# A two-layer hybrid encoder: down projection partly by seven block products, low weight products last in a block, wide weight tiles and one pool of general buffers

## The chip, the core and the metric

The kernel runs on one core of one Trainium2 chip, in one launch. The metric is device microseconds of one execution; the kernel before has a median of 1971.58 us over three runs (1971.37 to 1972.12). Engines are called TensorE (PE in the profile, its weight loads PEld), VectorE (DVE), ScalarE (ACT), GpSimd (POOL) and SyncE (SP).

## The reference

256 tokens of width 2048 go through two layers. Each layer normalises its rows, makes one input projection, runs windowed attention and a chunked spatial gate side by side, joins them by an output projection, and then runs a gated feed-forward part with a hidden width of 5632. All is float32. What the change concerns is the last line:

```python
def conv_gated_ffn(h, w_up, conv_w, conv_b, w_down):
    a = depthwise_conv_centred(h @ w_up, conv_w, conv_b)
    g, u = jnp.split(a, 2, axis=-1)
    return (jax.nn.silu(g) * u) @ w_down

x = x + conv_gated_ffn(rms_norm(x, norm2_g[l]), w_up[l], conv_w[l], conv_b[l], w_down[l])
```

## The kernel before

**Products in three parts.** TensorE multiplies in a rounded 32-bit format. To keep float32 accuracy, each operand is split into a rounded high part and the remainder, the low part, and a product is three matmuls into one PSUM sum: activation hi by weight hi, activation lo by weight hi, activation hi by weight lo. The activations (transposed, 128 x 128 for one of the two row halves m and one group of 128 channels k) are the operand that TensorE holds; 512 columns of weights stream past.

**A block.** The weights of every projection come as blocks of four k by 512 columns, 1 MB each. `split_weights` (L113) takes a raw tile from a pool of three, lets SyncE load it (L119), and has ScalarE copy it rounded into hi tiles (L127) and VectorE subtract these from raw into lo tiles (L111). Hi and lo tiles are 1024 wide, four of each; so each holds half a block, two blocks in all. `rows_by_cols` (L163) then issues 24 matmuls (L170): for each k four hi products (two row halves, activation hi and lo), then the two low products of the same k. In the very first blocks the raw tile is loaded in four pieces and split piece by piece.

**The feed-forward part.** `gate_and_up(j)` (L814) makes four k of the hidden activations: two sums of four blocks each, one for the gate and one for the up half. `leave` scales a finished sum, takes it apart into 16-bit halves, and SyncE transposes them by DMA (L809). Two `let_in` points later (there is one in each block, after its second k) the step after it runs: ScalarE puts the words together (L381, `together`), the convolution follows (L781 on ScalarE, L782 and L785 on VectorE), and for the up half the product with silu of the gate (L827) and the split of the hidden activations, `ys`, into hi (L242, ScalarE) and lo (L243, VectorE).

**The down projection.** The 44 k are handled in two parts, k 0 to 23 after six gate/up units, and k 24 to 43 after five more. In each part the four groups of 512 columns, c, come one after the other; each has a PSUM tile of two banks for the two row halves, goes through all blocks of the part, and is then added to the residual `xr` (`residual`, L560; in the last part of the last layer L872, from where it is written out). There are three such PSUM tiles (`mm`) and two of one bank (`tp`).

**What sets the order.** A scheduler places the instructions of each engine by priority and program order, and gives out pool buffers; splitting of weights is marked `urgent`, which lets it run as far ahead as buffers allow. On the chip each queue runs in its written order, and an instruction that reuses a buffer waits until the last reader of the old contents is done. General buffers: 58 slots `sl` of 512 words per partition, four `ev` and four `sc` of the same size.

## Time and profile before

| | before |
|---|---|
| median of three runs | 1971.58 us (1971.37 to 1972.12) |
| profiled execution | 1971.57 us, of which 1969.8 us are its span |
| granted TensorE clock | 1.000 |
| TensorE, busy | 1963.6 us |
| VectorE, busy | 1256.4 us |
| ScalarE, busy | 1316.6 us |
| bytes read | 378.43 MB |

The span reaches from the first to the last instruction of the profiled execution, and what lies around it is 1.8 us. Matmuls are pipelined: one takes 389 ns from its start to its end, while the next starts after less than 230, so busy time is the union and a rate is read from runs of matmuls. In a row of grouped instructions the two numbers behind the bar are busy time and the mean of one; "idle before" is what the engine stood still ahead of them.

### The profile page before, as it was taken

Reading aid. Unit: us, or ns where it says so; the run is one execution under the profiler, and the core shown is the slowest. Engines: PE = TensorE matmul, PEld = TensorE weight load, DVE = VectorE, ACT = ScalarE, POOL = GpSimd, SP = SyncE. Lnnn points to the kernel's source line nnn. Section 1 sums busy time; section 2 is a strip of 40 time slices with the busy share of each in tenths; the row PEclk is TensorE's granted clock in tenths of the full one; section 3 lists DMA queues with packets and bytes.
Section 4 is the critical chain, followed back from the end, with each engine's and each line's share of the span. In section 5 each row is a group of like instructions: output and inputs, shape, how many; then the busy total and the mean of one; then the engine's idle time right before and its main releaser. Section 6 shows DMA issues by size and latency. Waiting matters only on the chain.

```text
span 1969.8 us, 23916 instructions
## 1 busy us (share of the span) xinstructions
PE 1963.6 (100%) x8880; PEld 1630.6 (83%) x8880; DVE 1256.4 (64%) x1754; ACT 1316.6 (67%) x1685; POOL 22.6 (1%) x25
## 2 busy tenths in 40 slices
PE   9999999999999999999999999999999999999999
...
PEclk9999999999999999999999999999999999999999
...
GB/s 342 205 204 150 205 239 202 222 219 228 216 198 192 199 215 204 229 221 205 215 204 248 141 178 203 235 206 218 232 218 219 193 192 203 213 216 217 220 216 126
DMA packets 190741, 414.09 MB, mean 210 GB/s; under 512 B 139424, under 2 KB 140704, under 8 KB 145568
## 3 DMA queue, kind: packets, MB, share of 16 engines
...
q8 instruction: 69, 1.13, 0.2%
...
HBM read 378.43 MB, written 2.10 MB: 193 GB/s over the span
## 4 chain that ended last, share of the span: by engine, by line
PE 97%; DVE 2%; issue 0%; DMA 0%; SPq 0%; POOL 0%; ACT 0%; DVEq 0%
PE mm L170 91%; PE mm L211 2%; PE tp L170 1%; PE mm L216 1%; DVE lo L111 1%; PE tp L254 0%; PE tp L256 0%; PE tp L255 0%; PE tp L697 0%; PE tp L482 0%; DMA raw<-in_w_in 0%; DVE sl L235 0%; DVE xr L562 0%; SPq L87 0%; DVE sl L265 0%
## 5 line engine op out<-in xcount | busy, mean ns | idle before, releaser
L170 PE MATMUL mm<-hi,sl 128*128 128x512 f32 x5296 | 1418.4, 389 | 0.8 <-DVE sl L243 0.6
L111 DVE TENSOR_TENSOR lo<-raw,hi 128x1024 fp32r<-128x1024 f32 (+1 forms) x708 | 856.5, 1217 | 627.6 <-ACT hi L127 616.7
L170 PEld LDWEIGHTS mm<-hi,sl 128*128 128x128 f32 x5296 | 992.7, 188 | 208.2 <-DVE sl L243 1.5
L127 ACT ACTIVATE hi<-raw 128x1024 fp32r<-128x1024 f32 (+1 forms) x708 | 739.9, 1051 | 461.5 <-PE mm L170 426.0
L170 PE MATMUL mm<-lo,sl 128*128 128x512 f32 x2648 | 816.1, 389 | 0.0
L170 PEld LDWEIGHTS mm<-lo,sl 128*128 128x128 f32 x2648 | 496.9, 188 | 103.1
L381 ACT COPY sl<-sl 128x1024 uint16<-128x1024 uint16 x98 | 132.1, 1351 | 119.3 <-DMA sl<-sl 119.2
L781 ACT ACTIVATE sc<-sl,pc 128x256 f32<-128x256 f32 x176 | 97.0, 588 | 0.0
L801 ACT COPY sl<-ev 128x1024 uint16<-128x1024 uint16 x88 | 89.5, 1037 | 0.0
L782 DVE SCALAR_TENSOR_TENSOR sc<-sl,pc,sc 128x255 f32<-128x255 f32 x176 | 79.1, 479 | 2.6 <-ACT sc L781 2.6
L785 DVE SCALAR_TENSOR_TENSOR sc<-sl,pc,sc 128x255 f32<-128x255 f32 x176 | 79.1, 480 | 1.6
L211 PE MATMUL mm<-sl,hi 128*128 128x512 f32 x256 | 62.0, 391 | 0.0
L211 PEld LDWEIGHTS mm<-sl,hi 128*128 128x128 f32 x256 | 47.3, 188 | 9.3
L799 ACT ACTIVATE ev<-mm,yr 128x512 f32<-128x512 f32 x88 | 54.8, 672 | 0.0
L235 DVE SCALAR_TENSOR_TENSOR sl<-sl,pc 128x256 fp32r<-128x256 f32 x96 | 42.5, 479 | 16.9 <-ACT sl L234 16.9
L242 ACT ACTIVATE sl<-sl 128x256 fp32r<-128x256 f32 x88 | 32.1, 410 | 27.9 <-DVE sl L827 27.4
L234 ACT ACTIVATE sl<-sl,pc 128x256 fp32r<-128x256 f32 x96 | 43.0, 496 | 1.2 <-DMA pc<-in_pcol 0.6
L535 ACT COPY sl<-sl 128x1024 uint16<-128x1024 uint16 x24 | 32.4, 1349 | 6.8 <-DMA sl<-sl 6.8
L216 PE MATMUL mm<-sl,lo 128*128 128x256 f32 x256 | 34.2, 285 | 0.0
L243 DVE TENSOR_TENSOR sl<-sl 128x256 fp32r<-128x256 f32 x88 | 33.3, 419 | 0.0
L216 PEld LDWEIGHTS mm<-sl,lo 128*128 128x128 f32 x256 | 32.4, 191 | 0.6
L827 DVE TENSOR_TENSOR sl<-sl,sc 128x512 f32<-128x512 f32 x44 | 30.2, 686 | 0.2
...
## 6 DMA issues: line engine op xcount, KB each, us to landing
raw<-in_w_up SPq DMA_DIRECT2D x176, 1024.0 KB, 5.0
raw<-in_w_down SPq DMA_DIRECT2D x88, 1024.0 KB, 4.9
raw<-in_w_in SPq DMA_DIRECT2D x38, 1024.0 KB, 5.3
raw<-in_w_o SPq DMA_DIRECT2D x32, 1024.0 KB, 5.0
raw<-in_w_gu SPq DMA_DIRECT2D x16, 1024.0 KB, 5.1
sl<-sl SPq DMA_TRANSPOSE x244, 3.6
...
```

Source lines behind the costliest of these rows:

```text
L111: nc.vector.tensor_tensor(out=lo, in0=part, in1=hi.bitcast(F32), op=ALU.subtract)
L127: nc.scalar.activation(hi[:, cs], part, AF.Copy)
L170: nc.tensor.matmul(ps[m], acts[kk][:, part % 2, m * P : (m + 1) * P], w, start=first and kk == 0 and part == 0, stop=last and kk == KB - 1 ...
L211: nc.tensor.matmul(ps[:, i, :], tile_of(his, k, i), x1, start=k == 0, stop=False)
L216: nc.tensor.matmul(ps[:, i, :SEQ], tile_of(los, k, i), acts[k][:, 0, :], start=False, stop=k == NK - 1)
L234: nc.scalar.activation(t[:, 0, :], src, AF.Copy, scale=g)
L381: nc.scalar.copy(words, tall.rearrange("p (b a) n -> p b (a n)", b=2))
L781: nc.scalar.activation(t[:, i, :], s[:, i, :], AF.Identity, bias=col(3), scale=col(1))
L782: nc.vector.scalar_tensor_tensor(out=t[:, i, 1:], in0=s[:, i, : SEQ - 1], scalar=col(0), in1=t[:, i, 1:], op0=ALU.mult, op1=ALU.add)
L785: nc.vector.scalar_tensor_tensor(out=t[:, i, : SEQ - 1], in0=s[:, i, 1:], scalar=col(2), in1=t[:, i, : SEQ - 1], op0=ALU.mult, op1=ALU.add)
L799: nc.scalar.activation(rows, ps[:, m, :], AF.Copy, scale=r2[:, m : m + 1])
L801: nc.scalar.copy(h, rows.bitcast(U16).rearrange("p (j n b) -> p j b n", j=2, b=2))
```

## The change

**Seven products for eight.** Take two k (k0, k1), two column groups (c0, c1) and the two row halves: eight block products, 24 matmuls. In 20 places (ten per layer) of two k and two c each they are made by seven products of sums, 21 matmuls, in the scheme of Strassen and Winograd. `seven` loads the four 512-wide weight pieces as one raw tile; VectorE makes four sums of them in a second raw tile (three instructions); ScalarE makes hi parts of three pieces and of all sums, VectorE the low parts. `mixed` makes the four sums of activations on VectorE and splits them. Three of the seven products go into the PSUM sums of c0 and c1, and four kinds go into four extra sums `more` (one `mm` tile and both `tp` tiles), shared by all such blocks of a pair of c; `seven_out` adds these into `xr` at the end of the pair's last one.

**Where.** The parts are now k 0 to 19 (five gate/up units) and 20 to 43 (six). In the first part both pairs of c have such blocks at k 4, 8 and 14; in the second only the first pair has, at k 4, 8, 14 and 18 of the part. The two column groups of a pair now alternate block by block, and the seven-product block stands between them (the last one of the second part ahead of both).

**Elsewhere.** Hi and lo tiles are a whole block wide (2048), three hi and two lo; a block's 16 hi products come first and its eight low ones last; in the spatial gate's `unit` the low products go through k in the outer loop. `ev` and `sc` buffers come from the `sl` pool, which has 62. The weights of the down projection are laid out in the order of use.

The core of the diff:

```diff
+HALVES = ((0, 20), (20, NF))
+FAST = ((4, 8, 14), (4, 8, 14, 18))
...
-    slots = pool("slots", 58)
-    evp = pool("evp", 4)
+    slots = pool("slots", 62)
     rawp = pool("rawp", 3)
-    hip = pool("hip", 4)
-    lop = pool("lop", 4)
-    scr = pool("scr", 4)
+    hip = pool("hip", 3)
+    lop = pool("lop", 2)
...
+            hi, lo = hi_tile(), lo_tile()
+            for a in range(0, n, step):
+                cs = slice(a, min(a + step, n))
+                nc.scalar.activation(hi[:, cs], raw[:, cs], AF.Copy)
+                lo_part(lo[:, cs], raw[:, cs], hi[:, cs])
...
             for m in range(2):
                 product(m, kk, 0)
                 product(m, kk, 1)
-            for m in range(2):
-                product(m, kk, 2)
             if kk == 1:
                 let_in()
+        for kk in range(KB):
+            for m in range(2):
+                product(m, kk, 2)
...
+    def mixed(y):
+        t = y.rearrange("p a (m t) -> p (a m) t", t=P)
+        e = ev().rearrange("p a (m t) -> p (a m) t", t=P)
+        a21 = t[:, 1:2, :].to_broadcast([P, 2, P])
+        nc.vector.tensor_tensor(out=e[:, 0:2, :], in0=a21, in1=t[:, 0:4:3, :], op=ALU.subtract)
+        nc.vector.tensor_tensor(out=e[:, 2, :], in0=t[:, 0, :], in1=e[:, 1, :], op=ALU.subtract)
+        nc.vector.tensor_tensor(out=e[:, 3, :], in0=t[:, 2, :], in1=e[:, 2, :], op=ALU.subtract)
+        return parts(e.rearrange("p a t -> p (a t)"), [P, W])
+
+    def seven(left, right, more, acts, mix, src, used_left, used_right, first, last):
+        with urgent():
+            raw = raw_tile()
+            nc.sync.dma_start(raw, src)
+            sums = raw_tile()
+            hi, lo, his, los = hi_tile(), lo_tile(), hi_tile(), lo_tile()
+            nc.scalar.activation(hi[:, : 3 * W], raw[:, : 3 * W], AF.Copy)
...
+            nc.vector.tensor_tensor(out=s[:, 0:2, :], in0=b12, in1=b[:, 0:3:2, :], op=ALU.add)
+            nc.vector.tensor_tensor(out=s[:, 2, :], in0=s[:, 0, :], in1=b[:, 2, :], op=ALU.add)
+            nc.vector.tensor_tensor(out=s[:, 3, :], in0=s[:, 2, :], in1=b[:, 1, :], op=ALU.add)
+            nc.scalar.activation(his, sums, AF.Copy)
+            lo_part(lo[:, : 3 * W], raw[:, : 3 * W], hi[:, : 3 * W])
+            lo_part(los, sums, his)
...
+        product(left, used_left, 0, own(1, 0), (hi, lo), 1)
+        product(right, used_right, 0, mix_of(3), (hi, lo), 2)
+        product(more, used_more, 0, own(0, 0), (hi, lo), 0)
+        lows()
+        product(more, used_more, 1, mix_of(2), (his, los), 2)
+        product(more, used_more, 2, mix_of(1), (his, los), 0)
+        product(more, used_more, 3, mix_of(0), (his, los), 1)
+        product(left, used_left, 1, own(1, 1), (his, los), 3)
+        lows()
```

In the rows below, a name is a tile with its number, `out<-in`, and L is the line in the kernel that the rows are from: in the changed kernel L146 makes a low part, L253 to L255 the sums of weights, L238 to L240 those of activations, L367 the low part of these, L901 and L904 the convolution, L948 the product with the gate, L361 the low part of the hidden activations, L298 to L304 are `seven_out`, L678 is the residual, L213 a matmul of a plain block in the down projection, and L273, L274 and L279 are the hi and low matmuls of a seven-product block.

First, TensorE in layer 0 where the first part of the down projection has begun. Before, the first blocks of c0:

```order
L170 MATMUL mm_4683<-hi_4686,sl_3051 128x512 x4
L170 MATMUL mm_4683<-lo_4687,sl_3051 128x512 x2
L170 MATMUL mm_4683<-hi_4686,sl_3054 128x512 x4
L170 MATMUL mm_4683<-lo_4687,sl_3054 128x512 x2
L170 MATMUL mm_4683<-hi_4690,sl_3076 128x512 x4
L170 MATMUL mm_4683<-lo_4691,sl_3076 128x512 x2
L170 MATMUL mm_4683<-hi_4690,sl_3079 128x512 x4
L170 MATMUL mm_4683<-lo_4691,sl_3079 128x512 x2
```

Now, the first seven-product block, which follows the first plain block (lo_4051 is that plain block's low tile, hi_4089 and lo_4090 are the pieces, hi_4091 and lo_4092 the sums, sl_4027 and sl_4028 the mixed activations):

```order
L273 MATMUL mm_4047<-hi_4089,sl_3173 128x512
L274 MATMUL mm_4047<-hi_4089,sl_3173 128x512
L279 MATMUL mm_4047<-lo_4090,sl_3173 128x512
L273 MATMUL mm_4047<-hi_4091,sl_3173 128x512
L274 MATMUL mm_4047<-hi_4091,sl_3173 128x512
L279 MATMUL mm_4047<-lo_4092,sl_3173 128x512
L273 MATMUL mm_4082<-hi_4089,sl_4027 128x512
L273 MATMUL mm_4083<-hi_4089,sl_3170 128x512
L274 MATMUL mm_4083<-hi_4089,sl_3170 128x512
L279 MATMUL mm_4083<-lo_4090,sl_3170 128x512
L274 MATMUL mm_4082<-hi_4089,sl_4028 128x512
```

Where six matmuls with one pair of tiles stood, the sixth matmul takes the low part of the sums and the seventh the mixed activations.

Second, VectorE at the same place. Before:

```order
L111 TENSOR_TENSOR lo_4642<-raw_4635,hi_4641 128x1024
L782 SCALAR_TENSOR_TENSOR sc_4815<-sl_4657,pc_89,sc_4815 128x255 x2
L785 SCALAR_TENSOR_TENSOR sc_4815<-sl_4657,pc_89,sc_4815 128x255 x2
L111 TENSOR_TENSOR lo_4687<-raw_4684,hi_4686 128x1024
L111 TENSOR_TENSOR lo_4691<-raw_4684,hi_4690 128x1024
L111 TENSOR_TENSOR lo_4725<-raw_4722,hi_4724 128x1024
L111 TENSOR_TENSOR lo_4729<-raw_4722,hi_4728 128x1024
L111 TENSOR_TENSOR lo_4759<-raw_4756,hi_4758 128x1024
```

Now:

```order
L146 TENSOR_TENSOR lo_4090<-raw_4086,hi_4089 128x1536
L901 SCALAR_TENSOR_TENSOR sl_3989<-sl_3986,pc_83,sl_3989 128x255
L904 SCALAR_TENSOR_TENSOR sl_3989<-sl_3986,pc_83,sl_3989 128x255
L901 SCALAR_TENSOR_TENSOR sl_3989<-sl_3986,pc_83,sl_3989 128x255
L904 SCALAR_TENSOR_TENSOR sl_3989<-sl_3986,pc_83,sl_3989 128x255
L146 TENSOR_TENSOR lo_4092<-raw_4088,hi_4091 128x2048
L238 TENSOR_TENSOR sl_4023<-sl_3005 128x256
L239 TENSOR_TENSOR sl_4023<-sl_3005,sl_4023 128x128
L240 TENSOR_TENSOR sl_4023<-sl_3005,sl_4023 128x128
L367 TENSOR_TENSOR sl_4028<-sl_4023,sl_4027 128x512
```

Where low parts of whole blocks stood one behind the other, the mix's sums (sl_4023, which ScalarE rounds into sl_4027) stand behind lo_4092, the second lo tile of the seven-product block.

Third, VectorE from the end of the first pair in the first part to the first seven-product block of the second pair. Before, at the end of c0:

```order
L111 TENSOR_TENSOR lo_4948<-raw_4945,hi_4947 128x1024
L111 TENSOR_TENSOR lo_4952<-raw_4945,hi_4951 128x1024
L111 TENSOR_TENSOR lo_4982<-raw_4979,hi_4981 128x1024
L560 TENSOR_TENSOR xr_88<-mm_4683,xr_88 128x512 x2
L111 TENSOR_TENSOR lo_4986<-raw_4979,hi_4985 128x1024
L111 TENSOR_TENSOR lo_5016<-raw_5013,hi_5015 128x1024
L111 TENSOR_TENSOR lo_5020<-raw_5013,hi_5019 128x1024
```

Now (mm_4047 and mm_4082 are the sums of c0 and c1; lo_4428 belongs to the second pair's first plain block, raw_4459 to its first seven-product block):

```order
L302 TENSOR_TENSOR xr_82<-xr_82,sl_4343 128x512
L303 TENSOR_TENSOR xr_82<-xr_82,sl_4344 128x512
L146 TENSOR_TENSOR lo_4407<-raw_4404,hi_4406 128x1024
L304 TENSOR_TENSOR xr_82<-xr_82,sl_4345 128x2x512
L678 TENSOR_TENSOR xr_82<-mm_4047,xr_82 128x512 x2
L146 TENSOR_TENSOR lo_4428<-raw_4425,hi_4427 128x2048
L678 TENSOR_TENSOR xr_82<-mm_4082,xr_82 128x512 x2
L253 TENSOR_TENSOR raw_4461<-raw_4459 128x1024
L146 TENSOR_TENSOR lo_4463<-raw_4459,hi_4462 128x1536
L254 TENSOR_TENSOR raw_4461<-raw_4461,raw_4459 128x512
L255 TENSOR_TENSOR raw_4461<-raw_4461,raw_4459 128x512
L146 TENSOR_TENSOR lo_4465<-raw_4461,hi_4464 128x2048
```

The sums of weights stand behind the residuals of c0 and c1.

Fourth, VectorE in the second part of layer 0, at the last activations. Before:

```order
L782 SCALAR_TENSOR_TENSOR sc_7449<-sl_7267,pc_89,sc_7449 128x255
L785 SCALAR_TENSOR_TENSOR sc_7449<-sl_7267,pc_89,sc_7449 128x255
L111 TENSOR_TENSOR lo_7490<-raw_7483,hi_7489 128x1024
L782 SCALAR_TENSOR_TENSOR sc_7457<-sl_7446,pc_89,sc_7457 128x255 x2
L785 SCALAR_TENSOR_TENSOR sc_7457<-sl_7446,pc_89,sc_7457 128x255 x2
L111 TENSOR_TENSOR lo_7533<-raw_7530,hi_7532 128x1024
L827 TENSOR_TENSOR sl_7448<-sl_7448,sc_7457 128x512
L111 TENSOR_TENSOR lo_7537<-raw_7530,hi_7536 128x1024
L243 TENSOR_TENSOR sl_7465<-sl_7448,sl_7465 128x256
L243 TENSOR_TENSOR sl_7468<-sl_7448,sl_7468 128x256
```

Now (lo_7036 and lo_7038 belong to the last seven-product block, lo_7081 and lo_7123 to the plain blocks of c0 and c1 behind it, which take sl_6899, sl_6902, sl_6915 and sl_6918):

```order
L146 TENSOR_TENSOR lo_7038<-raw_7034,hi_7037 128x2048
L361 TENSOR_TENSOR sl_6899<-sl_6627,sl_6899 128x256
L361 TENSOR_TENSOR sl_6902<-sl_6627,sl_6902 128x256
L146 TENSOR_TENSOR lo_7081<-raw_7078,hi_7080 128x2048
L901 SCALAR_TENSOR_TENSOR sl_6907<-sl_6905,pc_83,sl_6907 128x255 x2
L904 SCALAR_TENSOR_TENSOR sl_6907<-sl_6905,pc_83,sl_6907 128x255 x2
L300 TENSOR_TENSOR xr_82<-xr_82,tp_6744 128x512
L948 TENSOR_TENSOR sl_6638<-sl_6638,sl_6907 128x512
L301 TENSOR_TENSOR xr_82<-xr_82,tp_6744 128x512
L146 TENSOR_TENSOR lo_7123<-raw_7120,hi_7122 128x2048
L361 TENSOR_TENSOR sl_6915<-sl_6638,sl_6915 128x256
L361 TENSOR_TENSOR sl_6918<-sl_6638,sl_6918 128x256
```

The low part sl_6915 of an activation stands behind two closing adds into `xr` and two low parts of whole blocks.

222 lines of the change are left out of this document (164 added, 58 removed).

## Prediction

> **What bounds the kernel now.** I read the page first (busy time, the slices, the chain that ended last), then the chain in order of time, the stage in question by windows, who waits for whom, and the durations by form.
>
> ```profile
> span 1969.8 us, 23916 instructions
> ...
> PE 1963.6 (100%) x8880; PEld 1630.6 (83%) x8880; DVE 1256.4 (64%) x1754; ACT 1316.6 (67%) x1685; POOL 22.6 (1%) x25
> PEclk9999999999999999999999999999999999999999
> ...
> PE 97%; DVE 2%; issue 0%; DMA 0%; SPq 0%; POOL 0%; ACT 0%; DVEq 0%
> PE mm L170 91%; PE mm L211 2%; PE tp L170 1%; PE mm L216 1%; DVE lo L111 1%; PE tp L254 0%; PE tp L256 0%; PE tp L255 0%; PE tp L697 0%; PE tp L482 0%; DMA raw<-in_w_in 0%; DVE sl L235 0%; DVE xr L562 0%; SPq L87 0%; DVE sl L265 0%
> ```
>
> TensorE is busy for 1963.6 of 1969.8 us, at full granted clock in every slice, and is 97% of the chain. Nothing ahead of it can be made shorter with profit; only fewer or shorter matmuls, or new gaps, move the end.
>
> ```profile
> 209.41 692.51 PE mm L170 x3055
> 901.96 0.38 DVE sl L243
> 1184.87 696.36 PE mm L170 x3072
> ```
>
> In the two long stretches 3072 matmuls take 696.36 us: 0.2267 us from one to the next, with no gap. The piece between is the kind of gap there is now: 0.38 us in which the chain runs through VectorE, which makes the low half of the last activations that the down projection wants.
>
> ```profile
> core 0: us, PE busy (x) PEld busy (x) DVE busy (x) ACT busy (x) POOL busy (x), PEclk, DMA share, GB/s
> 0.00:5.00 5.00, 3.95 (x18) 3.95 (x19) 0.97 (x3) 2.98 (x5) 1.66 (x9) 1.00 0.54 158
> 529.00:660.00 131.00, 131.00 (x580) 108.51 (x579) 69.60 (x73) 61.49 (x67) 0.00 (x0) 1.00 0.61 202
> ```
>
> The second stretch is layer 0's first down projection (24 blocks). VectorE is busy for 69.60 of its 131 us. That is the cover that the change spends.
>
> ```profile
> DVE lo L111 <- ACT hi L127: 616.7, 399, 6.2
> ACT hi L127 <- PE mm L170: 426.0, 302, 2.6
> ```
>
> VectorE's waits here are for ScalarE's hi parts, and ScalarE waits for TensorE to give back hi tiles: both run ahead of TensorE and wait for it, not the reverse.
>
> **The change part by part.** The durations that the sum uses:
>
> ```profile
> L170 PE MATMUL mm<-hi,sl 128*128 128x512 f32 x5296 | 1418.4, 389 | 0.8 <-DVE sl L243 0.6
> L111 DVE TENSOR_TENSOR lo<-raw,hi 128x1024 fp32r<-128x1024 f32 x700 | 851.1, 1223 | 625.5 <-ACT hi L127 614.7 <-PE mm L170 9.8 <-PE mm L216 0.4
> L127 ACT ACTIVATE hi<-raw 128x1024 fp32r<-128x1024 f32 x700 | 734.8, 1056 | 459.6 <-PE mm L170 426.0 <-PE tp L170 10.0 <-PE mm L211 6.7
> L381 ACT COPY sl<-sl 128x1024 uint16<-128x1024 uint16 x98 | 132.1, 1351 | 119.3 <-DMA sl<-sl 119.2
> L781 ACT ACTIVATE sc<-sl,pc 128x256 f32<-128x256 f32 x176 | 97.0, 588 | 0.0
> L785 DVE SCALAR_TENSOR_TENSOR sc<-sl,pc,sc 128x255 f32<-128x255 f32 x176 | 79.1, 480 | 1.6
> L782 DVE SCALAR_TENSOR_TENSOR sc<-sl,pc,sc 128x255 f32<-128x255 f32 x176 | 79.1, 479 | 2.6 <-ACT sc L781 2.6
> L827 DVE TENSOR_TENSOR sl<-sl,sc 128x512 f32<-128x512 f32 x44 | 30.2, 686 | 0.2
> L560 DVE TENSOR_TENSOR xr<-mm,xr 128x512 f32<-128x512 f32 x24 | 15.5, 686 | 10.7 <-PE mm L170 10.7
> L248 ACT ACTIVATE sl<-sl 128x512 fp32r<-128x512 f32 x10 | 6.3, 626 | 0.2
> L721 DVE TENSOR_TENSOR sl<-sl 128x512 f32<-128x512 f32 x8 | 5.5, 689 | 0.2
> L111 DVE TENSOR_TENSOR lo<-raw,hi 128x512 fp32r<-128x512 f32 x8 | 5.4, 692 | 2.0 <-ACT hi L127 2.0
> L127 ACT ACTIVATE hi<-raw 128x512 fp32r<-128x512 f32 x8 | 5.1, 633 | 1.9 <-DMA raw<-in_w_in 1.8
> L399 DVE TENSOR_TENSOR sl<-sl 128x256 f32<-128x256 f32 x4 | 1.7, 417 | 0.0
> L338 DVE TENSOR_TENSOR sl<-ropes,qk 128x128 f32<-128x128 f32 x8 | 2.3, 283 | 0.0
> ```
>
> *Fewer matmuls.* A block of 2 row halves, 2 k and 2 column groups was 8 products of 3 matmuls; it is 7 products, so 3 matmuls less. There are 20 such blocks (per layer 3 + 3 in the first part, 4 in the second). 60 x 0.2267 = 13.6 us less, all on the path, since nothing else is. This term is sure as long as the spacing holds. [...]
>
> *What a seven-product block asks of VectorE.* Adding up the weights (1024, 512 and 512 wide) is not in the trace; nearest are the equal tensor-tensor shapes, 1.22 + 0.69 + 0.69 = 2.6 us. Low parts: 512 more elements cost 1.223 - 0.692 = 0.53, so 1536 wide is 1.75 and 2048 wide 2.29. Together 6.6 us, where the same weights took 2 x 1.22 = 2.4. ScalarE: 512 more cost 0.42, so 1536 is 1.48 and 2048 is 1.90. In the first part VectorE now has 14 MB of plain weights x 2.29 = 32, six seven-blocks x 6.6 = 40, two closings of seven adds (6 x 0.69 + 1.22 = 5.4) = 11, three activation mixes (0.42 + 2 x 0.28 + 0.69 = 1.7) = 5, eight residual adds = 5.5, and about 5 that the window holds beside low parts and residuals today (69.6 - 24 x 2.45 - 5.5): 98 us. TensorE's time there is 462 x 0.2267 = 104.7. VectorE goes from half busy to nearly full, in an in-order queue; so each place where TensorE wants something early has to be gone through. S1, S2 ... are the seven-blocks in order, a seven-block takes 21 x 0.2267 = 4.76 us, a plain one 5.44; times count from the named moment.
>
> *S1, first part.* There are two lo tiles and S1 uses both, so its second one (of the summed weights) can be written only when the plain block before has ended, at 0. It is done at 2.3. TensorE wants it as its 6th matmul, at 1.13. Behind it on VectorE stand the adds of the first activation mix (0.42 + 0.28 + 0.28), then ScalarE's 0.63 for its hi part: 4.0 with the handing over. The 7th matmul wants that, at 1.36. Wait 2.7 us. Bounds: 1.2 if the mix were already there, 3.4 if its low part came last too. In the second part the same mix stands ahead of the lo tile and the matmuls are placed so that it comes as the 13th: about 0.
>
> *S2 and S3.* The summed low part is wanted as the 18th matmul, 3.86 after the start, and takes 2.3 from the start: 0, as long as VectorE reaches it in time. By the sums it does, with 1.5 to spare at S2 and almost none at S3.
>
> *S4, first part (first of the second pair).* Count from S3's end. VectorE still has 1.7 of the plain block's low part, then five of the closing adds and the sixth, 2 half-wide low parts (1.22 each), the last closing add (1.22), two residual adds (1.37), a low part (2.29), two residual adds, 1.22 of sums, the 1536-wide low part, and 2 x 0.69 of sums: 18.9. ScalarE's hi part of the sums makes it 20.8. TensorE has 24 + 12 + 12 + 24 + 9 matmuls until it wants that: 18.4. Wait 2.4. Bounds 0 (each instruction 0.1 less by overlap) and 4.
>
> *S4, second part, and the two plain blocks after it.* Weights take this long to come:
>
> ```profile
> raw<-in_w_down SPq DMA_DIRECT2D x88, 1024.0 KB, 4.9
> sl<-sl SPq DMA_TRANSPOSE x244, 3.6
> ```
>
> and the issue of four transposes this long on SyncE:
>
> ```profile
> 880.18 5.70 SPq L809 DMA_TRANSPOSE sl<-sl  x4
> ```
>
> The raw tile for this block is the one that S3's weights give back (three raw tiles, and a seven-block holds two). S1's start being 0, S3's low part (1.75) may start at 26, when the lo tile is free, and with the mix's adds before it is done at 28.3; so the load goes out then and lands at 33.2. Behind it in SyncE's queue stand the four transposes of the last gate/up tile: issued by 34.4, the first two by 31.5, so these land by 35.1, when ScalarE is about to copy them (34.7): 0 to 0.4. Then ScalarE: 1.48, the copy of the last gate/up tile 1.35, 0.59; VectorE's convolutions (4 x 0.48), sums, product (0.69) and low part, 7.0 in all: 43.6. TensorE wants it at 41.7 + 1.36. Wait 0.6 (0.2 to 1.2). The next two blocks take k 20 to 23, the last activations made. VectorE, after 43.6: low part of the sums 2.29, two y halves 0.84, low part 2.29, convolutions 1.92, a closing add 0.69, product 0.69, a closing add 0.69, low part of the second block 2.29, first y half 0.42: 55.7. TensorE could use that y 18 matmuls after the block's end (47.0): 51.1. Wait 4.5. Bounds: at least 1.9, since the second block's weights can be loaded only at 43.6 (+4.9, +1.90, +2.29, +0.42 = 53.1); at most 7.
>
> *The start.*
>
> ```profile
> 5.24 1.17 PE L170 MATMUL mm<-hi,sl 128*128 128x512 f32 x4
> 6.07 0.63 ACT L127 ACTIVATE hi<-raw 128x512 fp32r<-128x512 f32 x1 [1.03 <-DMA raw<-in_w_in]
> 7.86 0.63 ACT L127 ACTIVATE hi<-raw 128x512 fp32r<-128x512 f32 x1 [0.54 <-DMA raw<-in_w_in]
> 8.55 1.19 PE L170 MATMUL mm<-hi,sl 128*128 128x512 f32 x4
> ```
>
> The first weights come in four pieces. Now TensorE fills the time until the third (8.49) with the low products of the first two; with low products last these four matmuls are left over: +0.9 (0 to 1.5).
>
> *At nothing.* Plain blocks: wide tiles cost ScalarE and VectorE less (1.90 for 2.1, 2.29 for 2.45). The lo tile comes free only at a block's end, but is wanted 5.44 + 16 x 0.2267 = 9.1 us after that, against 2.29 of work; without that cover every plain block would pay. Fewer general buffers (62 for 66), the PSUM tiles that the extra sums take, the same weight bytes in another order: hidden behind the same running ahead; -1 (the few gaps of now) to +2. The halves' change from 24 + 20 to 20 + 24 k moves no count.
>
> *Sum.* Per layer 2.7 + 2.4 + 0.6 + 4.5 = 10.2, twice 20.4; with the start 21.3; less 13.6: +7.7. The profiled execution took 1971.57 us (span 1969.8), and the median is 1971.58, so 1979.3.
>
> **Rivals.**
> *The cover holds (faster).* VectorE and ScalarE keep so far ahead that only S1's tile wait in the first part is felt. For it: VectorE's overlap of neighbours could take about 0.05 to 0.1 us off each instruction, and queues of 25 instructions stand behind two of my waits. Against it: the load of the last block's weights bounds one of these at 1.9. 1971.6 - 13.6 + 0.9 + 5.4 = 1964.3. It decides if the two late chains together are under 1.6 us a layer.
> *Half of it.* S1 as above, the last blocks at their lower bound 1.9, S4 of the first part 0.5: 1971.6 - 13.6 + 0.9 + 2 x 5.1 = 1969.1; with the middle of the bounds, up to 1975: no change to speak of.
> *The clock falls.* Six waits of some us might let the clock drop.
>
> ```profile
> L98 PE MATMUL tp<-ones 128*128 128x128 f32 x20 | 4.4, 417 | 1.1 <-DVE ones L94 1.1
> L482 PE MATMUL tp<-ident,sl 128*128 128x128 f32 x64 | 9.3, 278 | 0.0
> ```
>
> The same 128 x 128 matmuls took 417 ns in the first five microseconds and 278 later, though the window's row shows a granted clock of 1.00 there. If the first 4.2 us after each long wait ran like that, each would cost 4.2 x (1 - 278/417) = 1.4, and six 8.4: 1987.7. [...] Against the rival: my waits are broken by single matmuls and none alone exceeds 2.7 us.
> *The change saves nothing* because the extra sums in PSUM or repeated row halves space the matmuls out: every matmul here already has its own weight load and all have one spacing, whatever the bank, so I give it next to nothing.
>
> **How the numbers follow.** The forecast's case has 0.54, half of it 0.15, the cover 0.19, the clock 0.12. The bound for a difference that a measurement of this kernel can tell is 0.2%, or 3.9 us. The forecast's own terms at their low ends (1.2 + 0 + 0.2 + 1.9 a layer, start 0.5) give 1965.1, at their high ends (3.4 + 4 + 1.2 + 7, start 1.5) 1990.7; 1964 to 1990 leaves out some of the cover's case and the worst of the clock's. Slower: most of the forecast's case and the clock's, 0.62; same 0.18; faster 0.2.
>
> **What would show it.** In the changed kernel's profile TensorE should have 60 matmuls less at the same 0.227, and idle time before matmuls of the seven-blocks and of the two plain blocks after the second part's fourth one, released by VectorE's low parts, by ScalarE's hi parts and by the split of the last activations: about 10 us a layer, most of it in those three places. VectorE should be busy for over 85% of the first down part. Wrong would be: no such idle time (then the cover held); idle time in the gate/up stretches (then the lo tiles are too few for plain blocks); a spacing other than 0.227, or a clock below full after the waits.

## The result and the profile after

The changed kernel takes 1993.83 us (median, 1990.8 to 1996.52), the kernel before 1971.53 beside it: a ratio of 1.0111, with an interval of 1.0096 to 1.0127. It is slower, as forecast, but by 22.3 us and not by 7.7. The profiled execution, from which all rows of this section are, took 1995.45 us.

The page of the changed kernel (busy time, granted clock by slices, the chain that ended last):

```profile
span 1993.6 us, 23002 instructions
PE 1964.6 (99%) x8820; PEld 1623.4 (81%) x8820; DVE 1355.6 (68%) x1594; ACT 1329.5 (67%) x1389; POOL 19.7 (1%) x25
PEclk9999999999999999999999999999999999999999
PE 89%; DVE 5%; ACT 3%; DMA 2%; issue 1%; SPq 0%; POOL 0%; DVEq 0%; ACTq 0%
```

The 60 matmuls are gone, and yet TensorE is busy for a microsecond longer than before: some of its matmuls ran slower (0.43 us apart at 507 us, for 0.2267). Its share of the chain fell from 97% to 89%; the rest went to VectorE, ScalarE and transfers, that is, to waits.

The first seven-block of layer 0 in the timeline (start, length, engine, line; in brackets the idle time before and its releaser). L273 and L274 are a product's two high matmuls, L279 its low one, L366 the high half of a mix, L240 the mix's last addition:

```profile
500.87 2.29 DVE L146 TENSOR_TENSOR lo<-raw,hi 128x2048 fp32r<-128x2048 f32 x1 [0.98 <-PE mm L213]
503.85 0.29 DVE L240 TENSOR_TENSOR sl<-sl 128x128 f32<-128x128 f32 x1
503.76 1.04 ACT L920 COPY sl<-sl 128x1024 uint16<-128x1024 uint16 x1
504.71 0.62 ACT L366 ACTIVATE sl<-sl 128x512 fp32r<-128x512 f32 x1
501.57 0.39 PE L274 MATMUL mm<-hi,sl 128*128 128x512 f32 x1
503.21 0.49 PE L279 MATMUL mm<-lo,sl 128*128 128x512 f32 x1 [1.25 <-DVE lo L146]
505.39 0.73 PE L273 MATMUL mm<-hi,sl 128*128 128x512 f32 x2 [1.68 <-ACT sl L366]
```

VectorE waits for the low tile that the plain block held, writes it, then makes the mix; TensorE waits for both in turn. Measured against a spacing of 0.2267 us the two waits are 1.41 and 1.95 us: 3.4, where 2.7 was forecast. ScalarE adds half a microsecond of that: copies of the up projection's sums (L920) stand in front of the mix's high half.

The last two plain blocks of the second part, behind S4:

```profile
924.33 2.12 PE L213 MATMUL mm<-hi,sl 128*128 128x512 f32 x8 [1.32 <-ACT hi L158]
927.41 0.73 PE L213 MATMUL mm<-hi,sl 128*128 128x512 f32 x2 [0.96 <-ACT sl L360]
929.10 1.48 PE L213 MATMUL mm<-hi,sl 128*128 128x512 f32 x3 [0.95 <-DVE sl L361]
```

The late weights and the late last activations stand there as forecast. What the forecast's sum did not have comes next: the windows of 2 us behind the two long waits of layer 0 (busy time of each engine, then the granted clock).

```profile
178.00:180.00 2.00, 0.96 (x2) 0.83 (x3) 2.00 (x6) 0.00 (x0) 0.00 (x0) 0.60 1.11 418
180.00:182.00 2.00, 2.00 (x6) 1.55 (x5) 2.00 (x7) 1.92 (x4) 0.00 (x0) 0.50 0.92 356
182.00:184.00 2.00, 2.00 (x6) 1.52 (x6) 0.69 (x2) 0.15 (x1) 0.00 (x0) 0.50 0.32 131
184.00:186.00 2.00, 2.00 (x12) 1.91 (x11) 0.38 (x2) 0.00 (x0) 0.00 (x0) 0.70 0.00 0
...
504.00:506.00 2.00, 0.61 (x3) 0.53 (x4) 0.78 (x3) 1.33 (x2) 0.00 (x0) 1.00 0.90 238
506.00:508.00 2.00, 2.00 (x7) 1.51 (x6) 1.19 (x5) 0.64 (x1) 0.00 (x0) 0.52 0.68 287
508.00:510.00 2.00, 2.00 (x7) 1.62 (x6) 2.00 (x1) 1.27 (x1) 0.00 (x0) 0.63 0.00 0
510.00:512.00 2.00, 2.00 (x10) 1.64 (x10) 1.30 (x2) 1.97 (x2) 0.00 (x0) 1.00 0.00 0
```

For 3.4 us at 506, and for twice that at 178, the clock is half, and six or seven matmuls stand in a window that has ten at full clock. The page's slices of 50 us round this away. There are two more such places (929 and 1492). TensorE's busy time times the missing part of the clock, summed over these windows, is 9.0 us.

The place at 178 us is in the attention and gating stage of layer 0, which has no seven-block. L347 adds up the two accumulator halves of a gating unit and so sets an accumulator free:

```profile
173.21 2.29 DVE L146 TENSOR_TENSOR lo<-raw,hi 128x2048 fp32r<-128x2048 f32 x1 [1.82 <-PE mm L334]
176.10 2.28 DVE L146 TENSOR_TENSOR lo<-raw,hi 128x2048 fp32r<-128x2048 f32 x1
178.30 0.69 DVE L347 TENSOR_TENSOR sl<-mm,sl 128x512 f32<-128x512 f32 x1
179.04 5.06 PE L185 MATMUL mm<-hi,sl 128*128 128x512 f32 x11 [3.51 <-DVE sl L347]
```

VectorE first waits 1.82 us for TensorE's last low products of the unit (L334) to give a low tile back, then writes two low tiles, and only then makes the small sum for which TensorE has stood still for 3.5 us. How late these sums are shows in the view of that one line. Changed kernel:

```profile
L347 DVE TENSOR_TENSOR sl<-mm,sl x4: 680/683/687, 154.8 to 196.0; 128x512 f32<-128x512 f32 x4
```

and the same line in the kernel before:

```profile
L229 DVE TENSOR_TENSOR ev<-mm,ev x4: 680/683/685, 132.0 to 176.6; 128x512 f32<-128x512 f32 x4
```

The first of the four sums comes 23 us later, though the stage begins only 3 us later. TensorE's wait ends with the second one, at 178.30 us; the experiment with a third low tile will show that the lateness of the first does no harm by itself.

The account of the profiled execution, 23.9 us over the one before: -13.6 for the matmuls; +19.4 of waits at and behind the sevens (S1 of the first part 6.7 for both layers, S4 of the first part 1.8, S1 of the second 2.4, S4 of the second 0.4, the plain blocks behind it 8.1, each as the distance between two starts less 0.2267 per matmul); +9.0 at half clock; +2.0 at the start; +6.0 of waits in the attention stages. That is 22.8; 1.1 are in no place of their own.

One part of the edit is not in the list of the change above: the convolution and the silu of the gate half are now made in a step of their own, when the gate's sums are ready, and no longer together with those of the up half. All kernels of the next section share it, save those made from the kernel before, as they share the new parts of 20 and 24 k, the one pool and the new order of the weights.

### The profile page after: what moved, and what is told of

Same layout as the page of the kernel before. It is cut to its first block, busy times and chain, and to the rows that moved or that the text cites. A ratio compares the mean times of both kernels' runs of the same rounds, so it can differ in the third digit from the quotient of the medians.

```text
span 1993.6 us, 23002 instructions
## 1 busy us (share of the span) xinstructions
PE 1964.6 (99%) x8820; PEld 1623.4 (81%) x8820; DVE 1355.6 (68%) x1594; ACT 1329.5 (67%) x1389; POOL 19.7 (1%) x25
## 4 chain that ended last, share of the span: by engine, by line
PE 89%; DVE 5%; ACT 3%; DMA 2%; issue 1%; SPq 0%; POOL 0%; DVEq 0%; ACTq 0%
PE mm L185 64%; PE mm L213 14%; PE mm L329 2%; DVE lo L146 2%; PE tp L213 2%; PE mm L334 1%; PE mm L273 1%; ACT hi L158 1%; PE mm L279 1%; PE mm L274 1%; DMA raw<-in_w_gu 1%; DMA sl<-sl 1%; ACT sl L499 0%; ACT hi L256 0%; DVE raw L253 0%
## 5 line engine op out<-in xcount | busy, mean ns | idle before, releaser
L146 DVE TENSOR_TENSOR lo<-raw,hi 128x2048 fp32r<-128x2048 f32 (+3 forms) x390 | 841.3, 2164 | 489.2 <-PE mm L185 357.1
L185 PE MATMUL mm<-hi,sl 128*128 128x512 f32 x3968 | 946.2, 390 | 5.7 <-DVE sl L347 3.5
L158 ACT ACTIVATE hi<-raw 128x2048 fp32r<-128x2048 f32 (+2 forms) x350 | 638.6, 1826 | 373.1 <-PE mm L185 173.1
L185 PEld LDWEIGHTS mm<-hi,sl 128*128 128x128 f32 x3968 | 745.0, 188 | 161.7 <-DVE sl L347 3.7
L185 PE MATMUL mm<-lo,sl 128*128 128x512 f32 x1984 | 491.7, 389 | 0.4 <-DVE lo L146 0.4
L213 PE MATMUL mm<-hi,sl 128*128 128x512 f32 x992 | 239.0, 391 | 6.5 <-ACT hi L158 2.8
L213 PEld LDWEIGHTS mm<-hi,sl 128*128 128x128 f32 x992 | 186.3, 188 | 47.9 <-ACT hi L158 3.6
L499 ACT COPY sl<-sl 128x1024 uint16<-128x1024 uint16 x98 | 132.3, 1350 | 125.0 <-DMA sl<-sl 125.0
L213 PE MATMUL mm<-lo,sl 128*128 128x512 f32 x496 | 123.5, 390 | 0.0
L213 PEld LDWEIGHTS mm<-lo,sl 128*128 128x128 f32 x496 | 93.5, 188 | 19.5
L901 DVE SCALAR_TENSOR_TENSOR sl<-sl,pc 128x255 f32<-128x255 f32 x176 | 80.3, 480 | 30.7 <-ACT sl L900 30.5
L900 ACT ACTIVATE sl<-sl,pc 128x256 f32<-128x256 f32 x176 | 95.7, 592 | 1.6
L920 ACT COPY sl<-sl 128x1024 uint16<-128x1024 uint16 x88 | 92.1, 1046 | 2.8
L904 DVE SCALAR_TENSOR_TENSOR sl<-sl,pc 128x255 f32<-128x255 f32 x176 | 77.5, 478 | 0.4
L256 ACT ACTIVATE hi<-raw 128x2048 fp32r<-128x2048 f32 x20 | 38.4, 1918 | 52.6 <-DVE raw L255 50.0
L918 ACT ACTIVATE sl<-mm,yr 128x512 f32<-128x512 f32 x88 | 59.7, 678 | 0.0
L273 PE MATMUL mm<-hi,sl 128*128 128x512 f32 x100 | 39.9, 406 | 6.9 <-ACT sl L366 5.4
```

What stands on the lines that cost most here:

```text
L146: nc.vector.tensor_tensor(out=lo, in0=part, in1=hi.bitcast(F32), op=ALU.subtract)
L158: nc.scalar.activation(hi[:, cs], raw[:, cs], AF.Copy)
L185: nc.tensor.matmul(ps[m], acts[kk][:, part % 2, m * P : (m + 1) * P], w, start=first and kk == 0 and part == 0, stop=last and kk == KB - 1 ...
L213: nc.tensor.matmul(ps[m], acts[kk][:, part % 2, m * P : (m + 1) * P], w, start=first, stop=done and kk == len(acts) - 1 and part == 2,)
L273: nc.tensor.matmul(ps[m], a[0], w[0][:, cs], start=new, stop=False)
L499: nc.scalar.copy(words, tall.rearrange("p (b a) n -> p b (a n)", b=2))
```

## The experiments

The theory at the outset: waits at the sevens, half clock behind them, and coarse low parts that hold up small VectorE steps in the attention stage. The rivals: all of it comes from the sevens; or all from the wide tiles. All times are medians beside the kernel before (1971.5 to 1971.9).

| kernel | us | ratio to before |
|---|---|---|
| changed kernel | 1993.83 | 1.0111 [1.0096, 1.0127] |
| no sevens | 1980.24 | 1.0044 [1.0029, 1.0059] |
| mixes early | 2043.09 | 1.0362 [1.0346, 1.0377] |
| half steps | 2003.83 | 1.0162 [1.0147, 1.0177] |
| no last seven | 1982.43 | 1.0051 [1.0034, 1.0068] |
| no sevens, three low tiles | 1976.51 | 1.0022 [1.0013, 1.0031] |
| sevens behind both plain blocks | 1992.88 | 1.0110 [1.0093, 1.0127] |
| three low tiles | 1976.73 | 1.0024 [1.0014, 1.0033] |
| four edits together | 1977.92 | 1.0031 [1.0019, 1.0043] |
| two mixes early | 1980.14 | 1.0039 [1.0026, 1.0052] |
| the same, no last seven | 1974.15 | 1.0009 [1.0000, 1.0018] |
| the same, no low half of the sums | 1974.31 | 1.0013 [1.0003, 1.0022] |
| the same, sums on GpSimd | 2017.46 | 1.0228 [1.0211, 1.0245] |
| two sevens in the middle, three low tiles | 1964.11 | 0.9959 [0.9945, 0.9974] |
| three sevens from the second group on | 1962.96 | 0.9954 [0.9937, 0.9970] |
| two sevens in the middle, two low tiles | 1971.10 | 0.9998 [0.9989, 1.0007] |

### No sevens

```diff
-FAST = ((4, 8, 14), (4, 8, 14, 18))
+FAST = ((), ())
```

> The changed kernel with no seven-products: every row of the down projection goes by plain blocks again (8880 matmuls, as before), while the wide tiles, 3 high and 2 low, the low products last and the one pool stay. The theory reads the excess of the changed kernel's profile by stage: some 2 us more at the start and some 8 to 9 us in the two attention and gating stages do not come from the sevens, so this kernel should take 1980 to 1984 us, still slower than before, with the stall of 3 to 4 us near 175 us and the half clock behind it still there, and no wait over 0.5 us in the down projections. The rival, that all of the loss comes from the sevens and that wide tiles and low products last cost nothing beyond the start, gives 1971.5 to 1974 us.

1980.24 us, as the theory had it. The stall of 3.5 us near 175 us and the half clock behind it (176 to 184 us) are there with no seven in the kernel, and no wait over 0.5 us is left in the down projections. So 8.5 us of the loss belong to what the change does beside the sevens (wide tiles, low products last and the rest), and 13.6 net to the sevens, which is 27.2 for their waits and clock once the 13.6 of saved matmuls are added.

### Mixes early

```diff
-                        plain[len(ys) - 2] = y
+                        plain[len(ys) - 2] = mixed(y)
...
-            mixes = {k: mixed(y) for k, y in plain.items()}
+            mixes = plain
```

> The changed kernel with the mixes of the activations made as soon as an activation pair exists, and not all together ahead of the down projection. The theory: the first wait of 3.4 us in the first seven-block of the first part is TensorE standing behind the mix, which stands in VectorE's queue behind the second low tile, and the half clock that follows is paid for it; so the wait falls from 3.4 to 1 us or less in each layer, the half clock after it is gone (some 1.4 us each or a little more), and the time falls by 6 to 9 us to 1985 to 1988 us. The rival, that the second low tile alone (2.2 us behind the first) sets that wait, leaves 2 us or more of it and the half clock, and 1992 to 1995 us.

2043.09 us: 49 us slower, neither theory. The timeline says why (L918 copies an up projection's accumulator out and so sets it free):

```profile
501.15 0.63 ACT L366 ACTIVATE sl<-sl 128x512 fp32r<-128x512 f32 x1 [3.27 <-DVE sl L240]
517.67 0.67 ACT L918 ACTIVATE sl<-mm,yr 128x512 f32<-128x512 f32 x1
520.05 0.79 PE L273 MATMUL mm<-hi,sl 128*128 128x512 f32 x1 [9.80 <-ACT sl L918]
```

ScalarE waits for an early mix, with the accumulator copies queued behind it; the seven then waits for an accumulator, four times for 3.6 and four for 9.2 to 9.8 us. The run does not tell whether the mix set the first wait; it shows that a step taken out of one engine's way can be put in another's.

### Half steps

```diff
-    def split_weights(src, loaded=None, step=4 * W):
+    def split_weights(src, loaded=None, step=2 * W):
...
-                raw=None, apart=False, step=4 * W):
+                raw=None, apart=False, step=2 * W):
```

(The two first kinds of block keep theirs, W and 2 W.)

> The changed kernel with every plain weight block split in two instructions of 1024 columns on ScalarE and VectorE in place of one of 2048, in the same wide tiles, so that only the length of an instruction in the queue changes and neither the number of tiles nor when a tile comes free. The theory is that the stall near 175 us is a small step (the sum of two accumulator halves, for the gates) that waits in VectorE's queue behind low parts of 2.2 us: with 1.1 us steps the stall falls from 3.5 us to 2 or less, the half clock behind it does not come, and the time falls by 4 to 8 us to 1986 to 1990 us. The rival is that a low tile which comes free only with its whole block is what delays: then the stall stays over 3 us and the time at 1992 to 1996 us.

2003.83 us, 10 slower than the changed kernel and outside both cases. At the stall:

```profile
172.57 4.63 DVE L146 TENSOR_TENSOR lo<-raw,hi 128x1024 fp32r<-128x1024 f32 x4 [1.90 <-PE mm L334]
177.12 0.68 DVE L347 TENSOR_TENSOR sl<-mm,sl 128x512 f32<-128x512 f32 x1
```

Four short low parts stand in front of the sum where two long ones stood, and all of them behind the same wait for a low tile. TensorE's stall there is 2.83 us for 3.51, neither the 2 or less of the theory nor the 3 or more of its rival, and this execution has no half clock behind it. So the length of a step has a small part in it; what is left points to the two blocks' low parts that are queued ahead of the sum and wait for tiles, which a later run tests. The 10 us come from elsewhere: low and high parts together (L146, L158) take VectorE 24 us and ScalarE 39 us longer, and the first seven of each part now waits 3.6 to 6.9 us.

### No last seven

```diff
-FAST = ((4, 8, 14), (4, 8, 14, 18))
+FAST = ((4, 8, 14), (4, 8, 14))
```

> The changed kernel without the fourth seven-block of the second part (k 18 and 19 of it by plain products), 3 matmuls more in the second part per layer and so 6 in all, 1.4 us. The theory is that the two plain blocks after that seven wait because ScalarE and VectorE, which made fourteen pieces for two seven-blocks close together, are behind there: the 5.8 and 4.1 us in those two blocks fall to under 1 us each, the half clock near 930 us is gone, and the time falls by 6 to 8 us net to 1986 to 1988 us. The rival is that the waits follow whichever seven is last in the part, by the closing sums that seven_out leaves: then they move with the third seven, and the time is 1994 to 1996 us.

1982.43 us, 11.4 less than the changed kernel. The waits in the two plain blocks (8.1 us in the profile) are gone, and no others came in their place: the theory's way, with more gain than expected. One seven, worth 0.7 us of TensorE in each layer, brought over 4 us of waits. The rest of the gain is clock, and not all of it this seven's: the stall near 175 us and the waits of S1 are as long as in the changed kernel, but this profile has one piece of 3.4 us at half clock behind the stall and one behind S1 of layer 1, where the changed kernel's has two each (and one more behind a wait of 1.9 us at 115 us).

### No sevens, three low tiles

On the kernel without sevens:

```diff
-    slots = pool("slots", 62)
+    slots = pool("slots", 58)
...
-    lop = pool("lop", 2)
+    lop = pool("lop", 3)
```

> No seven-products (as the first experiment, 1980.2 us), and three wide low tiles in place of two; the general pool gives the 8 KB for it and has 58 buffers, not 62. The theory, formed after half as long instructions had changed little: in the attention and gating stage the low parts of the next blocks stand in VectorE's queue and wait for one of two low tiles that TensorE still reads, and the small sums behind them (the sum of two accumulator halves that sets an accumulator free) wait as well. With a third tile the stall of 3.5 us near 175 us and the half clock behind it go, and the time is 1972.5 to 1975 us, of which 2 us are the start. The rival, that the order of the low products (all behind the high ones) sets the stall, leaves it, and 1979 to 1981 us.

1976.51 us: the stall near 175 us and its half clock are gone, as the second theory said. It is 1.5 us over the range: one new wait of 2.4 us in layer 1's first down projection (TensorE for a last activation), with half clock behind it.

### Sevens behind both plain blocks

```diff
-            own.insert(1 if i + KB < len(plain) else 0, (c, (k, k + 1), True))
+            own.insert(2 if i + KB < len(plain) else 0, (c, (k, k + 1), True))
```

> The changed kernel with each seven-block put behind both plain blocks of its group and not between them, so that the mixes and the sums of the first seven have 5.4 us more. The theory is that the first seven-block of a part waits for things that are still to be made in the queues at that point (mix, second low tile, last copies of the up projection's sums): its 3.4 us in the first part and 1.8 and 0.6 us in the second fall to 1.4 or less, without half clock after them, and the time is 1984 to 1988 us. The rival, that a seven's fourteen pieces take ScalarE and VectorE longer than the blocks in front cover wherever it stands, moves the waits along with it and gives 1991 to 1995 us.

1992.88 us, the rival. The waits of S1 fell to 0.8 us or less, but in the third group of plain blocks a wait of 4.4 us stands at 532 us and one at 1518 (TensorE for the split of the last activations, ScalarE L360), each with half clock behind it, and the sevens at the second part's end wait 2.4 us. The waits moved.

### Three low tiles, sevens and all

The two lines of the run without sevens, on the changed kernel.

> The changed kernel, sevens and all, with three wide low tiles and 58 general buffers. If two low tiles are what delays both the attention stage and the seven-blocks (a seven needs two of them at once), the stall near 175 us goes, the low tile's 1.4 us in the first seven of a part go, and the two plain blocks behind the last seven wait half as long: 1978 to 1983 us. If they delay the attention stage alone, only some 6 us go: 1986 to 1989 us. If fewer general buffers cost something, slower than that.

1976.73 us, better than either case: a third low tile, with four general buffers fewer, takes 17.1 of the 22.3 us away. The attention stage has no long stall: the first of the four gating sums is still late, at 152.2 us (132.0 before, 154.8 in the changed kernel), but the second comes 9.4 us earlier than in the changed kernel, and none is waited for.

```profile
168.91 0.69 DVE L347 TENSOR_TENSOR sl<-mm,sl 128x512 f32<-128x512 f32 x1
```

Besides, the second low tile no longer makes S1 wait, and the half clock fell from 9.0 to 3.4 us. What is left at S1, layer 0:

```profile
488.46 2.29 DVE L146 TENSOR_TENSOR lo<-raw,hi 128x2048 fp32r<-128x2048 f32 x1 [2.56 <-ACT hi L256]
490.67 0.42 DVE L238 TENSOR_TENSOR sl<-sl 128x256 f32<-128x256 f32 x1
491.65 1.91 ACT L158 ACTIVATE hi<-raw 128x2048 fp32r<-128x2048 f32 x1
493.46 0.61 ACT L366 ACTIVATE sl<-sl 128x512 fp32r<-128x512 f32 x1
494.13 0.73 PE L273 MATMUL mm<-hi,sl 128*128 128x512 f32 x2 [1.53 <-ACT sl L366]
```

The mix stands behind the second low tile, as the prediction had it, and its high half behind ScalarE's next weight block. The four S1 wait 1.7, 2.5, 2.6 and 1.0 us. The kernel is within 0.3 us of its twin without sevens: 13.6 us of saved matmuls still go into waits.

### Four edits together

Three low tiles, the seven behind both blocks, no last seven, and for the two blocks that come in pieces:

```diff
                 product(m, kk, 1)
+            if raw is not None:
+                for m in range(2):
+                    product(m, kk, 2)
...
-        for kk in range(KB):
+        for kk in range(KB if raw is None else 0):
```

> The changed kernel with four edits together: three low tiles and 58 general buffers; each seven behind both plain blocks; no fourth seven in the second part; and in the two first blocks, whose weights come in four pieces, the low products of a piece right behind its high ones, as in the kernel before. It has 8826 matmuls, 54 fewer than before, 12.2 us at 0.2267. If the waits found so far are all that eats the gain, 1.8 us for the closing sums of the first part stay and perhaps 2 more: 1961 to 1966 us, faster than both kernels. If seven-blocks bring waits wherever they stand, 1970 us or more.

1977.92 us, the rival. At the start TensorE's gaps are nearly those of the kernel before again (some 1.5 us regained), but the third group of plain blocks waits 2.9 us for the last activations in both layers, with half clock behind it, at S4 of the first part a plain block waits 1.8 and 2.2 us for the residual sums, and S1 of layer 1 waits 2.3 us for the high half of its mix. The long waits stand where they stood in the run that put the sevens behind both blocks, only shorter.

### Two mixes early, with and without the last seven

Three low tiles, the order at the start as above, and

```diff
-                        plain[len(ys) - 2] = y
+                        plain[len(ys) - 2] = mixed(y) if len(ys) < 11 else y
...
-            mixes = {k: mixed(y) for k, y in plain.items()}
+            mixes = {k: y if k < 9 else mixed(y) for k, y in plain.items()}
```

> As the kernel with three low tiles (1976.7 us), and two edits more: the mixes of the first two sevens of a part (k 4 and 8) are made as soon as their activations exist, those of the later ones where the change makes them; and the two first blocks take the low products of each piece right behind its high ones. The theory is that TensorE's waits in the first seven of each part (1.7, 2.5, 2.6 and 1.0 us, each ending with the high half of the mix on ScalarE, which comes behind VectorE's second low tile and ScalarE's next weight block) are the mix alone: they and the half clock that follows two or three of them go, some 9 to 10 us, and 1 us at the start: 1965 to 1968 us, faster than both kernels. The rival, taken from the earlier try that made all mixes early and cost 49 us, is that mixes made early push ScalarE's copies of the up projection's sums back, so that the first seven waits for an accumulator instead: 1976 us or more.

1980.14 us, the rival's range, 3.4 us slower than with three low tiles alone: the waits of S1 for its mix are gone in all four parts, and no time with them. The rival's mechanism is small here: only in the second part does the seven wait for an accumulator, 0.7 us in each layer. In the first part the plain block next to S1 waits instead, 2.5 and 1.4 us, for its high part. In the second kernel of the pair the fourth seven is dropped as well.

> As the run before it, and no fourth seven in the second part: 6 matmuls more, 1.4 us, against the waits of 1.4 and 1.2 us that the kernel with three low tiles shows in the plain block behind that seven. If those waits and nothing else go, the two are equal within 2 us of each other. If the last seven's sums also delay the blocks behind it in ways the trace puts down to other steps, this one is faster by 3 us or more.

1974.15 us, 6.0 faster than its twin, the second case. In the twin the last seven itself waits 1.8 us in each layer for the high half of its sums, and there are shorter waits ahead of that: 7.9 us in all and one half clock of 1.7, where this kernel has 2.6 us of waits in those places; the 1.4 us of matmuls go the other way. Where the wait for the mix was, both kernels wait for something else. This one, layer 0, where its own half clock follows:

```profile
499.48 1.09 ACT L903 ACTIVATE sl<-sl,pc 128x256 f32<-128x256 f32 x2
500.48 1.90 ACT L158 ACTIVATE hi<-raw 128x2048 fp32r<-128x2048 f32 x1
502.43 4.84 PE L216 MATMUL mm<-hi,sl 128*128 128x512 f32 x13 [2.62 <-ACT hi L158]
```

The plain block behind S1 now waits for its high part, which stands in ScalarE's queue behind the convolutions (L903) of the last activations.

### No low half of the sums

On the kernel just told (without the fourth seven):

```diff
-            hi, lo, his, los = hi_tile(), lo_tile(), hi_tile(), lo_tile()
+            hi, lo, his = hi_tile(), lo_tile(), hi_tile()
+            los = lo
...
-            lo_part(los, sums, his)
+            lo_part(lo[:, 3 * W :], sums[:, 3 * W :], his[:, 3 * W :])
```

> The run before last (1974.2 us: three low tiles, two mixes early, no fourth seven), but the low half of a seven's four weight sums is left out, so that VectorE makes a low part of 512 columns there and not of 2048 (some 1.6 us less for each of 18 sevens), and TensorE multiplies the same number of times with the low tile of the plain weights in its place; that part of the product is wrong by the low half. If VectorE's load near the sevens sets the waits, those of the down projections (some 13 us with the half clock) fall by half or more and the time is 1965 to 1969 us. If the waits come from the order of the queues on ScalarE (its weight blocks behind the last activations), 1972 to 1975 us.

1974.31 us: unchanged, the second case. With 1.6 us less of VectorE in each seven, and one low tile less, the wait of 2.6 us behind S1 is the same. So VectorE's load does not set what is left. That the order in ScalarE's queue near the first seven does is read from the trace; no run changed that order alone.

### Sums on GpSimd

On the kernel without the fourth seven (1974.15 us), with all low parts, `nc.gpsimd` in place of `nc.vector` for the three sums of weights.

> The run before last (1974.2 us), with the four weight sums of each seven made on GpSimd, which is idle 99% of the time, and not on VectorE: 2.6 us less for VectorE in each of 18 sevens, with the full result. No run here shows what GpSimd takes for a sum of 1024 columns. If it is done in 5 us or less for the three instructions and VectorE's load is what sets the waits, 1965 to 1970 us; if the sums come late instead, the last four products of each seven wait and the time is over 1976 us.

2017.46 us, the second case by its time, but not by its mechanism.

```profile
L256 POOL TENSOR_TENSOR raw<-raw 128x1024 f32<-128x1024 f32 x18 | 45.0, 2503 | 1176.6 <-DVE lo L146 450.5 <-DVE sl L904 305.6 <-DVE sl L364 264.4
L257 POOL TENSOR_TENSOR raw<-raw 128x512 f32<-128x512 f32 x18 | 32.1, 1783 | 1.4
L258 POOL TENSOR_TENSOR raw<-raw 128x512 f32<-128x512 f32 x18 | 27.6, 1533 | 1.4
```

The three sums take 5.8 us and not VectorE's 2.6. The long waits are not those of a seven's last products for the sums: four of together 23.5 us are of a seven's high matmuls (L276) for the accumulator copies (ScalarE L921), 13.7 us are lost at half clock, and why the copies come so late was not followed up.

### Two sevens in the middle

Three low tiles, the order at the start, and

```diff
-FAST = ((4, 8, 14), (4, 8, 14, 18))
+FAST = ((8, 14), (8, 14))
...
-        if i // KB < len(fast):
-            k = f0 + fast[i // KB]
+        if 0 <= i // KB - 1 < len(fast):
+            k = f0 + fast[i // KB - 1]
```

> Three low tiles, low products of the four pieces at the start right behind the high ones, and two sevens in each pair of columns (k 8 and 14) in place of three or four, in the second and third group of plain blocks, so that none stands in the first group, where the last activations are still being made, and none at the end. 12 sevens, 36 matmuls fewer than before, 8.2 us. If what is left of the waits belongs to the first seven of a part (the mixes and the last activations are late there) and to the last (the closing sums and late blocks), 1965 to 1969 us, faster than both kernels. If every seven brings its wait of some 0.7 to 1 us wherever it stands, what it saves (0.7 us) is lost again, and the time is 1973 to 1976 us.

1964.11 us, a little under the first case's range: faster than both kernels, 0.9959 [0.9945, 0.9974] of the one before. Page, and the first down projection of layer 0:

```profile
span 1962.3 us, 22806 instructions
PE 1955.9 (100%) x8844; PEld 1623.1 (83%) x8844; DVE 1310.8 (67%) x1534; ACT 1320.1 (67%) x1373; POOL 20.5 (1%) x25
```

```profile
488.00:600.00 112.00, 112.00 (x496) 92.74 (x495) 87.78 (x84) 58.41 (x46) 0.00 (x0) 1.00 0.62 211
```

TensorE has no gap there, while VectorE is nearly as busy (87.78 of 112 us, 78%) as in the changed kernel's same stage (91.94 of 111 us, 83%):

```profile
495.00:606.00 111.00, 107.33 (x464) 87.77 (x463) 91.94 (x93) 61.76 (x52) 0.00 (x0) 0.98 0.60 198
```

8.2 us of matmuls were saved and 7.8 arrived. So all that this kernel shares with the changed one beside the sevens (the new parts, the one pool, the order of the weights, the gate's own step, and, once there are three low tiles, wide tiles and low products last save at the start) costs some 0.4 us together.

### Three sevens from the second group on

As the run before, with `FAST = ((4, 8, 14), (4, 8, 14))`.

> As the kernel with two sevens in the middle groups (1964.1 us), with a third (k 4 too), so that the sevens stand in the second, third and fourth group of plain blocks of a part, none in the first; 18 sevens, 54 matmuls fewer than before. The third saves 18 matmuls, 4.1 us. If only the first group is dear, 1960 to 1962 us. If the last group of the first part (which has two plain activations left and the closing sums behind it) brings waits too, 1963 to 1966 us; if the loss comes from the number of sevens and not from their place, 1972 us or more.

1962.96 us, between the first two cases: the lowest median of the study, though its interval and that of the kernel with two sevens overlap. Its profile has one wait over 1 us in the down projections, 2.4 us at 1490 us, with half clock behind it. It is in the third group of plain blocks of layer 1's first part, for the split of a last activation, and not in the last group, as the second case had it. The kernel has as many sevens as the two of 1974 us and as many low tiles (the one without the low half of the sums uses one fewer in each seven); they differ in two mixes made early there, and in the first group of plain blocks, free of sevens here. No run has these tiles and as many sevens from the first group on without the early mixes. As an estimate: the kernel with three low tiles, which makes no mix early, is 13.8 us slower; the order at the start is worth some 1.5 of that and a last seven 6.0 (the pair above), so some 6 us are left for the first group, if such differences may be added.

### Two sevens in the middle, two low tiles

The changed kernel with nothing but the diff of the kernel with two sevens in the middle.

> The changed kernel, two low tiles and 62 general buffers, with nothing altered but the sevens: two in each pair of columns (k 8 and 14) in the second and third group of plain blocks. It parts the two causes found. If the place and the number of the sevens set the waits in the down projections, and the low tiles those of the attention stage, the down projections run without waits over 1 us, the stall of 3.5 us near 175 us stays, and the time is 1971 to 1975 us (1964.1 and some 8 us of the attention stage, and 1 at the start). If two low tiles also make the sevens wait wherever they stand, 1978 us or more.

1971.10 us, the first case. The down projections have no wait over 0.35 us, so two low tiles do not make sevens wait in the middle groups; the stall of 3.5 us near 175 us is there.

### Waits put into the kernel before

```diff
+                if c and not end:
+                    with urgent():
+                        a = sc([P, W])
+                        w = xr[:, 0, : W // 2]
+                        nc.vector.tensor_tensor(out=a[:, : W // 2], in0=held[0][:, : W // 2], in1=w, op=ALU.add)
...
+                        nc.vector.tensor_tensor(out=ps[0][:, : W // 2], in0=a[:, : W // 2], in1=w, op=ALU.add)
+                held = ps
```

What the chain writes is overwritten by the column's first matmul.

> The kernel before, with waits put in: ahead of eleven of the down projection's columns VectorE runs a chain of 2 to 12 small additions that starts from the column before and ends with a write into the accumulator of the next, so that TensorE waits some 1 to 6 us there. It measures by itself the disputed cost, the half clock behind a wait. My prediction held that no wait under 2.7 us would bring it; in the changed kernel and the experiments it stands behind single waits of 2.4 us and up, and behind pairs such as 1.4 and 1.9 us, and not behind 1.8 us. If that reading is right, waits of 2.0 us and less are followed by 0.2267 us spacing at once and those of 2.4 us and more by some 3 to 7 us at half speed, each costing 1.4 us or more on top. The rival, that pieces at half clock come at random, shows no such point.

The eleven waits came out at 3.4 to 7.9 us, longer than meant. Each was followed by half clock, for 3.4 us four times and for 6.8 us seven times: 2054.72 us in one execution, of which 59 are the waits and 23 the clock. None was short, so the chain was put ahead of the residual sum, with one to three additions of 32 to 512 columns.

> The kernel before with shorter waits put in than in the run that put in 3.4 to 7.9 us, every one of which was followed by half clock: one to three additions of 32 to 512 columns on VectorE between a column of the down projection and the next, ahead of the sum into the residual, for waits of some 0.7 to 3 us. If half clock needs a wait of a certain length, the waits under it are followed by none and those above by 3 to 5 us of it; the runs so far have none behind single waits of 1.9 us and less, and some behind 2.4 to 2.8 us. If it comes at random, some of the short ones have it as well.

This run's clock was 0.75 from end to end (2477.32 us), and tells nothing of a full clock:

```profile
PEclk7777777777777777777777777777777777777777
```

> The same kernel as in the last run (the kernel before with short waits put in), since that run was at three quarters of the clock from end to end and so shows little of what a wait does to a full clock. As there: waits of some 0.7 to 3 us; if half clock needs a certain length, none behind those under it and 3 to 5 us of it behind those above.

1994.86 us. Behind a wait of 2.04 us (at 1624) and one of 2.84 (at 967):

```profile
968.00:970.00 2.00, 0.00 (x0) 0.00 (x0) 2.00 (x5) 1.28 (x3) 0.00 (x0) 0.93 0.02 8
970.00:972.00 2.00, 1.80 (x4) 1.49 (x5) 1.18 (x2) 2.00 (x5) 0.00 (x0) 0.50 0.33 66
972.00:974.00 2.00, 2.00 (x8) 1.58 (x7) 0.00 (x0) 0.11 (x2) 0.00 (x0) 0.71 0.44 89
...
1624.00:1626.00 2.00, 0.58 (x3) 0.16 (x1) 1.38 (x3) 1.06 (x1) 0.00 (x0) 1.00 0.59 250
1626.00:1628.00 2.00, 1.54 (x7) 1.31 (x8) 1.44 (x3) 0.00 (x0) 0.00 (x0) 1.00 0.00 0
```

The seven waits from 0.55 to 2.04 us had no half clock behind them, the four of 2.31, 2.39, 2.71 and 2.84 us each had 3.4 us of it, 1.5 to 1.7 us lost. It is not random, and it needs no wait of 2.7 us.

What decides here can be read from all the profiles together. In one execution the pieces at half clock begin at whole multiples of 3.4133 us from each other: in the changed kernel at 178.39, 506.07, 929.32 and 1492.52 us, that is 327.68, 423.25 and 563.20 us apart, or 96, 124 and 165 times 3.4133. Cut every profile but the one at 0.75 into stretches on this grid, and leave out the first 10 us and the last 2. Then 58 stretches at full clock are followed by one at half clock, and in each of the 58 TensorE is busy for 1.64 us or less of the 3.41. Of the more than 10,000 other stretches at full clock three have less than that (1.47, 1.54 and 1.58 us). A stretch at half clock is followed by a second one where TensorE is busy in it for 2.76 us or less, and by full clock where it is busy for 2.82 or more. So in these profiles not the length of one wait decides, but how long TensorE stands still within one stretch. The same wait behind S1, 2.62 and 2.58 us long, in the kernel without the fourth seven and in the one without the low half of the sums:

```profile
499.59:503.01 3.42, 0.80 (x4) 0.49 (x4) 2.83 (x6) 3.42 (x5) 0.00 (x0) 1.00 0.00 0
503.01:506.42 3.41, 3.41 (x10) 2.63 (x9) 2.61 (x4) 3.14 (x4) 0.00 (x0) 0.50 0.25 41
...
497.96:501.37 3.41, 1.65 (x8) 1.03 (x6) 3.27 (x7) 3.38 (x5) 0.00 (x0) 1.00 0.00 0
501.37:504.79 3.42, 2.60 (x11) 2.16 (x12) 2.90 (x3) 3.39 (x5) 0.00 (x0) 1.00 0.00 0
504.79:508.20 3.41, 3.41 (x16) 2.83 (x16) 1.33 (x4) 3.38 (x4) 0.00 (x0) 1.00 0.78 269
```

In the first it falls into one stretch, with 0.80 us of matmuls, and half clock follows; in the second it is divided between two, with 1.65 and 2.60 us, and the clock stays full. In the same way two short waits count together, as 1.41 and 1.95 us at S1 of the changed kernel do (1.18 us of matmuls in the stretch from 502.66 us, half clock in the next). And a stall of one length can bring one piece or two: the one of 3.5 us near 175 us brings two in four of the kernels that have it and one in two others.

## Why the prediction was wrong

*Fewer matmuls*: right. 8820, and 0.2267 us apart wherever nothing waited and the clock was full.

The profiled execution is 23.9 us over the one before, 16.2 more than forecast: 9.0 of it is half clock, 6.0 are waits in the attention stages, 1.1 the start, and 1.1 have no place; the waits at the sevens came out 1.0 under.

*The waits at the sevens*: right in mechanism; the sum, 19.4 us for 20.4, is near by luck, since errors of the parts cancel. S1 of the first part 3.4 a layer for 2.7 (ScalarE's copies ahead of the mix were not seen); S4 of the first part 0.9 for 2.4; S1 of the second part 1.8 and 0.6 for about 0; S4 of the second part and the blocks behind it 4.0 and 4.5 for 5.1. VectorE's 98 us in the first part measured 92, which is 83% and not the 85% or more that was named as a sign.

*At nothing*: the step that failed first. "The lo tile comes free only at a block's end, but is wanted 9.1 us after that" holds for a plain block whose low part is made just behind the last one. In the gating units of the attention stage two wide tiles are held through a unit, and VectorE's queue had two blocks' low parts ahead of the sum of an older unit. (The sign that the prediction named, idle time in the gate/up stretches, did not come; the low tiles ran short in another stage.) The cover was measured against the next low part and not against the small steps queued behind it. Measured: 6.0 us of waits and 2.98 of the 9.0 us of half clock. The third tile took the stall away, and half as long steps only brought it from 3.5 to 2.8 us, so it is the number of tiles and the order in the queue far more than the length of an instruction.

*The clock*: the other step that failed, left out of the sum, and named as a rival at 8.4 us; it was 9.0. The argument against it, that waits are broken by single matmuls and none alone exceeds 2.7 us, was the author's estimate of what is short enough: after the first 10 us the trace of the kernel before has no gap between matmuls of 0.4 us or more, so it shows no such length. It failed twice: a wait of 3.5 us stood in a stage where none was expected, and 2.31 us was enough in the kernel with short waits, as were 1.41 and 1.95 here with a few matmuls between. 7.7 with the rival's 8.4 would have been 16.1 of the 22.3. That 8.4 and 9.0 are so near is luck: the rival had six waits at the sevens and 1.4 us each; there are four places, one of them without a seven, with six pieces of up to 1.7 us. The half clock came in pieces of 3.4 us, here one or two, on a grid of 3.4133 us, and no wait had to last a whole step of it: four waits of 2.3 to 2.9 us brought it, as did every stretch of the grid with less than 1.4 us of matmuls. Five waits of 2.3 to 2.9 us in other kernels were without it, because they were divided between two stretches or fell on the edge of 1.5 to 1.6 us.

*The start*: mis-sized, 2.0 for 0.9. The low products last left three gaps, not four matmuls; the old order at the start took most of them away.

What the experiments say of the cause: of the 22.3 us two low tiles are worth 17.1 with the sevens of the change in place, their share of the half clock included (no sum over edits: with sevens in the middle groups the tile and the start together are worth 7.0). The rest goes with the place of the first and the last seven: without sevens in the first group and at the end the matmuls' saving arrives. In the first group ScalarE's and VectorE's queues still hold the last activations, and each edit there (mixes early, seven later, less low part) only changed which step TensorE waited for. That VectorE is nearly full, on which the forecast rested, is not in itself the cause: it is at 78% in the kernel of 1964 us, without a gap, for 83%. Not settled: how much of the last kernels' gain is the place of the sevens and how much that no mix is made early; whether the place of the grid in an execution, which differs from profile to profile (a step begins at 499.24 us in the changed kernel's and at 499.59 in that of the kernel without the fourth seven), is why the changed kernel's runs spread over 5.7 us and those of the kernel before over 0.8. That the low products last have a part of their own in the attention stage was not tried apart from the tiles; with three of them the first gating sum is still 20 us later than before, without a wait.
